# Residual stream turned to tokens on the partitions in a two-layer decoder trunk

## The chip, the core and the metric

The kernel runs on one NeuronCore of a Trainium2 chip. The core has engines that run side by side, each with a queue of its own: TensorE (PE in the profile; PEld is its loading of the stationary operand) multiplies matrices and writes to PSUM, VectorE (DVE) and ScalarE (ACT) do elementwise work, GpSimd (POOL) fills small tiles and can issue transfers, and SyncE (SP) issues transfers (DMA) between HBM and the on-chip memory SBUF. Engines wait for each other through semaphores. SBUF has 128 partitions; a tile is written here as partitions x elements. PSUM has eight banks of 512 fp32 numbers per partition, and here a bank holds one running sum.

A matrix product has a *stationary* operand of at most 128x128, which is loaded into the array, and a *moving* operand of up to 512 columns, which streams past it. The metric is device microseconds (us) of one execution; lower is better.

## The reference

A decoder trunk of two layers on 256 tokens of width 2048, all fp32. What matters here:

```
ALPHA = (2 * DEPTH) ** 0.25

def short_conv_mixer(x, w_in, conv_w, w_out):
    bcu = x @ w_in
    gate_b, gate_c, u = jnp.split(bcu, 3, axis=-1)
    v = gate_c * u
    y = lax.conv_general_dilated(...)
    return (gate_b * y) @ w_out

def sq_relu_mlp(x, w1, w2):
    return jnp.square(jax.nn.relu(x @ w1)) @ w2

for layer in range(DEPTH):
    if layer < N_A:
        mix = short_conv_mixer(h, ...)
    else:
        if layer == N_A:
            k_nope, k_pe, v = shared_latent_kv(h, ...)
        mix = mla_mixer(h, ..., k_nope, k_pe, v, cos, sin)
    h = layer_norm(ALPHA * h + mix, ln_g[layer, 0], ln_b[layer, 0])
    h = layer_norm(ALPHA * h + sq_relu_mlp(h, mlp_w1[layer], mlp_w2[layer]),
                   ln_g[layer, 1], ln_b[layer, 1])
return h
```

There is one layer of each kind, so there are four layer norms (0 to 3): after the convolution mixer, after the first MLP, after attention, after the second MLP. The MLP's hidden width is 8192. `w_out` (2048x2048), `w_o` (2048x2048) and the two `w2` (8192x2048) are called down projections here: their results are added to the residual stream.

## The kernel before

**Precision.** Every fp32 operand `a` of a large product is split into `hi`, a copy rounded to a faster format, and `lo = a - hi`; a product is the sum of hi·hi, hi·lo and lo·hi. ACT makes `hi` by a cast (L112 for weights, L198 for activations) and DVE makes `lo` by a subtraction (L113, L199). An activation tile has `hi` of 256 tokens in columns 0 to 255 and `lo` in columns 256 to 511.

**Layout.** Activations and the residual stream have features on the partitions and tokens in the columns: `xres` is 128 x 16 x 256. The stationary operand is a 128x128 weight block and the activations move. A *pair* (`mm_run`, L133 and L137) is one product of 512 columns (`hi` of the weight with both halves of the activation) and one of 256 (`lo` of the weight with `hi` of the activation); `mm` (L151 to L153) does the same in three products of 256 columns with one result of 256. Only the value projection of attention (L590 to L592) holds the activations (128 tokens) and moves 512 weight columns, three products for each block of inputs.

**Weights** come as one stream of 712 halves of 128x1024 (512 KB). `take` hands out the next halves and asks for splitting four halves ahead (`LOOK`). A half is loaded by SP into one of five `raw` buffers and split into one of eight `hi` and `lo` buffers (`whl`), which come free when the last product that reads them has ended.

**Order.** The program is written in one sequence; a scheduler of the framework orders the instructions of each engine, by the order of the text among those that are ready as it reckons, and places the semaphores. Each engine then runs its own list in that order and waits where an operand isn't ready. PSUM banks are taken from two pools of four, by turns: `Banks.next` counts the requests and takes the pool `pmm` where the count modulo 8 is under 4 and the second pool otherwise.

**Stages.** Convolution mixer (48 units of `w_in`); `w_out` with norm 0; the first MLP in eight eighths (`NQ`), each of 8 units of `w1` and then the down projection of these 1024 hidden features for all 2048 outputs; the key, value and query latents (9 units); attention in four groups of four heads, with the projections of the next group interleaved and the first units of `w_o` beside the last; the rest of `w_o` with norm 2; the second MLP; norm 3 and output.

**Layer norm before.** While outputs of a down projection are added to `xres` (`add`, L354, after `residual`), each 128-feature chunk is counted into running sums (`count`) and at once scaled by its gain and split into `xd` (`wide`, L286 and L287), not yet normalised. The next stage's first products, `mm_wide` (L164 to L166, 258 columns: 256 tokens and the gain and bias columns), start on `xd`. Mean and variance come from small products (`stats`, L296), and the normalisation is applied to the results of the products (`weighted`, L343 to L345), beside the normalising of `xres` itself (`normal`, L331 to L336). To keep numbers small a mean over the first chunk is subtracted beforehand (`prepare`, `mu0p`, L256). At the end (`to_out`) chunks are transposed on PE (L707) and normalised with a last product (L739).

## Time and profile before

| | us |
|---|---|
| median of 3 runs | 2080.92 (2079.13 to 2081.73) |
| the profiled execution | 2080.19 |
| its span, first to last instruction | 2078.4 |
| mean granted TensorE clock | 0.998 of full |

The profile is of one execution. Its page lists, for each engine, the time that it was busy and its share of the span; a chain of waits, which is followed back from the last instruction to what released each step; and groups of instructions, one line each: source line, engine, operation, output<-inputs, partitions x elements, how many, then busy time, mean ns of one, and idle time of the engine just before them with what ended it. A table of stretches gives, for each stretch `from:to` in us, its length and the busy time of each engine with the number of instructions, then the granted clock, the share of the DMA engines and GB/s. A timeline row is: start us, duration us, engine, line, operation, tiles, form, count. Products of PE are pipelined: one starts before the one ahead has left the array, so distances between starts are prices and durations are not.

### The profile page before, as it was taken

Reading aid. Unit: us, or ns where it says so; the run is one execution under the profiler, and the core shown is the slowest. Engines: PE = TensorE matmul, PEld = TensorE weight load, DVE = VectorE, ACT = ScalarE, POOL = GpSimd, SP = SyncE. Lnnn points to the kernel's source line nnn. Section 1 sums busy time; section 2 is a strip of 40 time slices with the busy share of each in tenths; the row PEclk is TensorE's granted clock in tenths of the full one; section 3 lists DMA queues with packets and bytes.
Section 4 is the critical chain, followed back from the end, with each engine's and each line's share of the span. In section 5 each row is a group of like instructions: output and inputs, shape, how many; then the busy total and the mean of one; then the engine's idle time right before and its main releaser. Section 6 shows DMA issues by size and latency. Waiting matters only on the chain.

```text
span 2078.4 us, 32534 instructions
## 1 busy us (share of the span) xinstructions
PE 2068.4 (100%) x12640; PEld 1841.6 (89%) x12640; DVE 1512.2 (73%) x2490; ACT 1010.8 (49%) x1473; POOL 2.2 (0%) x21
## 2 busy tenths in 40 slices
PE   9999999999999999999999999999999999999998
PEld 8888888988888888888899998898888888888898
DVE  7667677886676767667788878788667676676776
ACT  6444445654444443444456665565444444444354
POOL 0000000000000000000000000000000000000000
PEclk9999999999999999999999999999999999999999
DMA  8555555555555556565555444556555555555551
GB/s 312 196 186 189 190 185 188 176 193 187 191 191 193 188 179 202 190 189 190 192 183 173 133 142 143 188 167 202 190 188 190 193 190 187 192 192 190 188 183 62
DMA packets 107447, 383.42 MB, mean 184 GB/s; under 512 B 11927, under 2 KB 13335, under 8 KB 107287
## 3 DMA queue, kind: packets, MB, share of 16 engines
q1 hardware_dynamic: 107148, 381.09, 56.1%
q8 instruction: 99, 1.62, 0.3%
q14 instruction: 56, 0.45, 0.1%
q10 hardware_dynamic: 144, 0.26, 0.0%
HBM read 379.20 MB, written 2.10 MB: 183 GB/s over the span
## 4 chain that ended last, share of the span: by engine, by line
PE 98%; DVE 1%; DMA 0%; ACT 0%; issue 0%; DVEq 0%; ACTq 0%
PE ps_u L133 51%; PE ps_u L137 25%; PE ps_g L133 3%; PE ps_w L166 2%; PE ps_w L164 2%; PE ps_w L165 2%; PE ps_g L137 1%; PE ps_u L152 1%; PE ps_u L151 1%; PE ps_u L153 1%; PE S L612 0%; DMA xres<-in_xT_dram 0%; PE S L611 0%; PE ps_q L153 0%; PE ps_q L152 0%; PE ps_q L151 0%
## 5 line engine op out<-in xcount | busy, mean ns | idle before, releaser
L112 ACT CAST hi<-raw 128x1024 fp32r<-128x1024 f32 x712 | 747.7, 1053 | 909.1 <-PE ps_u L133 775.6
L113 DVE TENSOR_TENSOR lo<-raw,hi 128x1024 fp32r<-128x1024 f32 x712 | 870.4, 1224 | 366.6 <-ACT hi L112 344.0
L133 PE MATMUL ps_u<-xhl,hi 128*128 128x512 f32 x2512 | 874.8, 394 | 0.0
L137 PE MATMUL ps_u<-xhl,lo 128*128 128x256 f32 x2512 | 698.0, 278 | 0.0
L133 PEld LDWEIGHTS ps_u<-xhl,hi 128*128 128x128 f32 x2512 | 471.1, 188 | 110.1
L133 PE MATMUL ps_u<-h,hi 128*128 128x512 f32 x1568 | 544.2, 394 | 0.0
L137 PEld LDWEIGHTS ps_u<-xhl,lo 128*128 128x128 f32 x2512 | 472.2, 188 | 0.1
L137 PE MATMUL ps_u<-h,lo 128*128 128x256 f32 x1568 | 434.3, 277 | 0.0
L133 PEld LDWEIGHTS ps_u<-h,hi 128*128 128x128 f32 x1568 | 294.0, 188 | 68.3
L137 PEld LDWEIGHTS ps_u<-h,lo 128*128 128x128 f32 x1568 | 294.3, 188 | 0.0
L354 DVE TENSOR_TENSOR xres<-xres,ps_u 128x256 f32<-128x256 f32 x422 | 177.2, 420 | 116.2 <-PE ps_u L137 99.9
L166 PE MATMUL ps_w<-xd,hi 128*128 128x258 f32 x400 | 113.3, 284 | 0.0
L164 PE MATMUL ps_w<-xd,hi 128*128 128x258 f32 x400 | 113.2, 283 | 0.0
L165 PE MATMUL ps_w<-xd,lo 128*128 128x258 f32 x400 | 112.9, 282 | 0.0
L133 PE MATMUL ps_u<-z,hi 128*128 128x512 f32 x256 | 90.6, 399 | 0.0
L133 PE MATMUL ps_g<-h,hi 128*128 128x512 f32 x224 | 78.3, 394 | 0.0
L164 PEld LDWEIGHTS ps_w<-xd,hi 128*128 128x128 f32 x400 | 76.3, 191 | 0.1
L166 PEld LDWEIGHTS ps_w<-xd,hi 128*128 128x128 f32 x400 | 75.7, 190 | 0.0
L165 PEld LDWEIGHTS ps_w<-xd,lo 128*128 128x128 f32 x400 | 75.2, 188 | 0.0
L133 PE MATMUL ps_u<-oT,hi 128*128 128x512 f32 x208 | 73.5, 399 | 0.0
L137 PE MATMUL ps_u<-z,lo 128*128 128x256 f32 x256 | 71.7, 281 | 0.0
L198 ACT CAST h<-fh 128x256 fp32r<-128x256 f32 x128 | 51.5, 402 | 36.6 <-DVE fh L431 36.6
(211 smaller groups left out, 2091.2 us busy)
## 6 DMA issues: line engine op xcount, KB each, us to landing
raw<-in_w_dram SPq DMA_DIRECT2D x512, 512.0 KB, 4.1
raw<-in_w_in_dram SPq DMA_DIRECT2D x90, 512.0 KB, 3.4
raw<-in_w_out_dram SPq DMA_DIRECT2D x32, 512.0 KB, 3.3
raw<-in_w_o_dram SPq DMA_DIRECT2D x32, 512.0 KB, 3.4
raw<-in_w_kv_dram SPq DMA_DIRECT2D x10, 512.0 KB, 4.2
raw<-in_w_q_dram SPq DMA_DIRECT2D x8, 512.0 KB, 3.4
raw<-in_w_uk_dram SPq DMA_DIRECT2D x8, 512.0 KB, 3.3
raw<-in_w_qn_dram SPq DMA_DIRECT2D x8, 512.0 KB, 3.3
```

The lines of the kernel that those rows point to most:

```text
L112: nc.scalar.copy(hi[:, at, :], rv)
L113: nc.vector.tensor_tensor(lo[:, at, :], rv, hi[:, at, :].bitcast(F32), ALU.subtract)
L133: nc.tensor.matmul(ps, w[blk // 8][0][:, blk % 8, :], x, start=first, stop=False)
L137: nc.tensor.matmul(ps[:, :T], w[blk // 8][1][:, blk % 8, :], x[:, :T], start=False, stop=last)
L151: nc.tensor.matmul(ps[:, :T], lo, x[:, :T], start=first, stop=False)
L152: nc.tensor.matmul(ps[:, :T], hi, x[:, T:], start=False, stop=False)
L153: nc.tensor.matmul(ps[:, :T], hi, x[:, :T], start=False, stop=last)
L164: nc.tensor.matmul(ps[:, :W], hi, xd[:, k, :W], start=k == 0, stop=False)
L165: nc.tensor.matmul(ps[:, :W], lo, xd[:, k, :W], start=False, stop=False)
L166: nc.tensor.matmul(ps[:, :W], hi, xd[:, k, W:], start=False, stop=k == NC - 1)
L198: nc.scalar.copy(dst[:, :T], src)
L354: nc.vector.tensor_tensor(d, d, ps[:, :T], ALU.add)
```

## The change

- The residual stream is `res`, 128 tokens x 2 halves x 2048 features; it is loaded from a second copy of the input, by POOL, during the convolution.
- Down projections (`down`) hold the activations and move the weights: for each block of 512 output features (`NB` = 4) and each half of the tokens (`t`) one bank sums `dot`s of three products of 512 columns. Weights are laid out for it (`_rows`); the number of halves is the same. In the last block of the last down projection before a norm, the last four weight halves are held (`TAIL`), and token half 0 is summed before token half 1.
- `Norm.behind` adds a finished bank to `res` and takes statistics of the 512 columns with `bn_stats`; after the fourth block `finish` makes mean and reciprocal deviation per token. `normal` normalises 512 columns in place: one ACT operation and two on DVE with gain and bias, which POOL broadcasts to all partitions by DMA (`gb`).
- Before the next up projection, `turned` normalises, transposes on PE and splits each 128 x 512 block, and after both token halves of a block runs its 4 x 3 pairs for the first three weight units (`group_of(GROUP)`).
- `mm_wide`, `xd`, `weighted`, `prepare`, `count`, `stats`, `spread` of the norms and `to_out` are gone. The latents use ordinary pairs and `whole`.
- The last eighth's down projection no longer uses the three products of 256 columns, and `w_o`'s part beside attention is one block of 512 outputs in place of three units of 128.
- The first three weight units come in one transfer for each cut (`w_first`), `xT` chunks are split two at a time, and four constants are loaded by POOL.

```diff
+CUTS = (0, 2, 4, 8, 12, 16)
+TAIL = 4
+    def group_of(n, nk=NC):
+        return [(take(nk // 8), psum("ps_g")) for _ in range(n)]
+    def dot(ps, w, kk, x, k, t, nk):
+        hi, lo = (v[:, 4 * kk:4 * kk + 4, :].rearrange("p a c -> p (a c)") for v in w)
+        xh, xl = (x[:, k, o + t * P:o + (t + 1) * P] for o in (0, T))
+        nc.tensor.matmul(ps, xh, hi, start=k == 0, stop=False)
+        nc.tensor.matmul(ps, xh, lo, start=False, stop=False)
+        nc.tensor.matmul(ps, xl, hi, start=False, stop=k == nk - 1)
+
+    def down(x, nk, put, blocks=range(NB), last=False):
+        for n in blocks:
+            ps = [psum("ps_d") for _ in range(2)]
+            late = TAIL if last and n == NB - 1 else 0
+            for j in range(nk // 2 - late):
+                w, = take(1)
+                for kk in range(2):
+                    for t in range(2):
+                        dot(ps[t], w, kk, x, 2 * j + kk, t, nk)
+            ws = [take(1)[0] for _ in range(late)]
+            for t in range(2):
+                for i, w in enumerate(ws):
+                    for kk in range(2):
+                        dot(ps[t], w, kk, x, nk - 2 * late + 2 * i + kk, t, nk)
+                put(n, t, ps[t])
...
+    res = act.tile([P, 2, D], F32, tag="res", name="res")
+    def first_add(n, t, ps):
+        nc.vector.scalar_tensor_tensor(block(n, t), block(n, t), ALPHA, ps, ALU.mult, ALU.add)
+    def add(n, t, ps):
+        nc.vector.tensor_tensor(block(n, t), block(n, t), ps, ALU.add)
     class Norm:
-        def prepare(self, m):
-        def count(self, m):
-        def widen(self):
-        def wide(self, m):
-        def stats(self):
-        def weighted(self, ps, f):
...
+        def __init__(self, idx):
+            self.idx = idx
+            self.stats = small.tile([P, 2, NB, 6], F32, tag="stats", name=f"stats{idx}")
+            self.gb = act.tile([P, NB, 2 * BW], F32, tag="c", name=f"gb{idx}")
+            for n in range(NB):
+                nc.gpsimd.dma_start(self.gb[:, n, :], gb[idx, n].partition_broadcast(P))
+            self.rn = {}
+        def behind(self, put):
+            def go(n, t, ps):
+                put(n, t, ps)
+                nc.vector.bn_stats(out=self.stats[:, t, n, :], in_=block(n, t))
+                if n == NB - 1:
+                    self.finish(t)
+            return go
+        def finish(self, t):
+            mv = small.tile([P, 2], F32, tag="mv", name="mv")
+            nc.vector.bn_aggr(out=mv, in_=self.stats[:, t, :, :])
+            ve = small.tile([P, 1], F32, tag="ve1", name="ve1")
+            nc.vector.tensor_scalar(ve, mv[:, 1:2], LN_EPS, None, ALU.add)
+            rn = small.tile([P, 2], F32, tag="rn", name="rn")
+            rsqrt(rn[:, 0:1], ve)
+            nc.vector.scalar_tensor_tensor(rn[:, 1:2], mv[:, 0:1], -1.0, rn[:, 0:1], ALU.mult, ALU.mult)
+            self.rn[t] = rn
+        def normal(self, n, t):
+            r, g, b = block(n, t), self.gb[:, n, :BW], self.gb[:, n, BW:]
+            rn = self.rn[t]
+            u = tmp.tile([P, BW], F32, tag="u", name="u")
+            nc.scalar.activation(u, r, AF.Identity, bias=rn[:, 1:2], scale=rn[:, 0:1])
+            nc.vector.tensor_tensor(u, u, g, ALU.mult)
+            nc.vector.tensor_tensor(r, u, b, ALU.add)
+        def turned(self, dst, ws):
+            for n in range(NB):
+                for t in range(2):
+                    self.normal(n, t)
+                    ps = psum("turned")
+                    for j in range(4):
+                        nc.tensor.transpose(ps[:, j * P:(j + 1) * P], block(n, t)[:, j * P:(j + 1) * P], id_t)
+                    at = slice(4 * n, 4 * n + 4)
+                    hi, lo = (dst[:, at, o + t * P:o + (t + 1) * P] for o in (0, T))
+                    split(hi, lo, ps.rearrange("p (j c) -> p j c", c=P))
+                mm_run(ws, dst, 4 * n, 4 * n + 4, NC)
...
-    summed(ln, products(NC, z), residual, ln.wide)
+    ln = Norm(0)
+    down(z, NC, ln.behind(first_add), last=True)
+    def mlp(idx, ln):
         xhl = act.tile([P, NC, 2 * T], F32R, tag="b", name=f"xhl{idx}")
+        ws = group_of(GROUP)
+        ln.turned(xhl, ws)
         for q in range(NQ):
-            h = act.tile([P, QC, 2 * T], F32R, tag="c", name=f"h{idx}_{q}")
+            h = act.tile([P, QC, 2 * T], F32R, tag="a", name=f"h{idx}_{q}")
+            for m, ps in enumerate(products(QC, xhl, ws=() if q else ws)):
...
+            if q < NQ - 1:
+                down(h, QC, add if q else first_add)
             else:
+                ln = Norm(idx)
+                down(h, QC, ln.behind(add), last=True)
+        return ln
...
+    ln = Norm(2)
+    put = ln.behind(first_add)
+    for t in range(2):
+        put(0, t, first_o[t])
     banks = Banks.open("second")
+    down(oT, H, put, blocks=range(1, NB), last=True)
+    ln = mlp(3, ln)
+    for t in range(2):
+        for n in range(NB):
+            ln.normal(n, t)
+            nc.sync.dma_start(out[t * P:(t + 1) * P, n * BW:(n + 1) * BW], block(n, t))
```

467 lines of the change are left out of this document (110 added, 357 removed).

## The prediction

> **What bounds the kernel now.** I read the page's engine table and chain of waits first, then the groups of PE instructions, then the table of stretches, one stretch for each stage of the code.
>
> ```profile
> span 2078.4 us, 32534 instructions
> PE 2068.4 (100%) x12640; PEld 1841.6 (89%) x12640; DVE 1512.2 (73%) x2490; ACT 1010.8 (49%) x1473; POOL 2.2 (0%) x21
> PE 98%; DVE 1%; DMA 0%; ACT 0%; issue 0%; DVEq 0%; ACTq 0%
> L133 PE MATMUL ps_u<-h,hi 128*128 128x512 f32 x1568 | 544.2, 394 | 0.0
> ```
>
> TensorE (PE) is never idle and is 98% of the chain, so a change is worth what it does to PE's sequence: how long each product takes, and whether PE must ever stand still. The 394 ns of a product is its passage through a pipeline, not its price; prices have to come from starts and from stretches.
>
> ```profile
> core 0: us, PE busy (x) PEld busy (x) DVE busy (x) ACT busy (x) POOL busy (x), PEclk, DMA share, GB/s
> 277.10:367.70 90.60, 90.60 (x515) 78.36 (x514) 68.70 (x111) 46.60 (x65) 0.00 (x0) 1.00 0.56 186
> 367.70:415.20 47.50, 47.50 (x399) 47.50 (x398) 39.31 (x75) 31.61 (x55) 0.00 (x0) 1.00 0.54 173
> 503.90:548.30 44.40, 44.40 (x259) 38.83 (x258) 32.82 (x49) 17.45 (x18) 0.00 (x0) 1.00 0.61 190
> 1036.80:1082.90 46.10, 46.10 (x387) 46.10 (x386) 41.43 (x78) 28.27 (x48) 0.00 (x0) 1.00 0.56 183
> 1082.90:1136.80 53.90, 53.90 (x453) 53.90 (x452) 45.75 (x89) 34.96 (x63) 0.00 (x0) 1.00 0.55 177
> 1346.50:1393.90 47.40, 47.40 (x399) 47.40 (x398) 39.61 (x75) 31.76 (x55) 0.00 (x0) 1.00 0.55 178
> 2015.60:2063.50 47.90, 47.90 (x402) 47.75 (x402) 33.81 (x59) 23.44 (x42) 0.00 (x0) 1.00 0.17 57
> ```
>
> In order: the `w_out` product; the first "wide" group (norm 0, with the statistics inside it); one ordinary down projection of an MLP eighth (128 pairs of one 512-column and one 256-column product); the last eighth's down projection in three 256-column products; the nine wide latent units; the wide group of norm 2; the last down projection of all. PE is full in each: **the norms cost the old kernel no standstill**, because the products start on un-normalised columns.
>
> **Part one, down projections.** Per four 128x128 weight blocks the old form has eight products and 3072 moving columns, the new one six of 512 columns, the same 3072. The new form is in the trace already, in the value projection (L590 to L592); two starts of its second column block:
>
> ```profile
> 1149.18 0.39 PE L592 MATMUL ps_v<-hi,lat 128*128 128x512 f32 x1
> 1153.95 0.39 PE L592 MATMUL ps_v<-hi,lat 128*128 128x512 f32 x1
> ```
>
> They lie 21 products apart: 4.77/21 = 0.2271 us each. So an eighth costs 192 x 0.2271 = 43.6 against 44.4 (saves 0.8, 14 times: 11.2); the two last eighths 43.6 against 46.1 and 47.9 (2.5 + 4.3); `w_out` 384 x 0.2271 = 87.2 against 90.6 (3.4), `w_o` taken like it (3.4). **Saved: 24.8.** The other bound is the neighbouring form's rate, 44.4/192 = 0.2313: then only the last eighths and the two long products gain, 24.8 - 3840 x 0.0042 = 8.7.
>
> **Part two, wide products.** They become ordinary pairs, 128 for 44.4 us, 144 for 49.9: saves 47.5 - 44.4, 47.4 - 44.4 and 53.9 - 49.9 = **10.1**. The centring products on the ones matrix go too:
>
> ```profile
> L256 PE MATMUL mu0p<-xres,ones 128*128 128x256 f32 x8 | 2.5, 391 | 0.0
> ```
>
> Between 0 and 2.5, taken 1.3, since the durations of neighbours overlap.
>
> **Part three, three norms in the open.** In the new `mlp` and before the latents, PE has nothing to do between the last product of a down projection and the first transposed block: `turned` needs the finished statistics. The rows nearest to its steps (512 columns, of which some are known at 256 or 1024):
>
> ```profile
> L112 ACT CAST hi<-raw 128x1024 fp32r<-128x1024 f32 x712 | 747.7, 1053 | 909.1 <-PE ps_u L133 775.6 <-issue 65.2 <-PE ps_g L133 19.8
> L113 DVE TENSOR_TENSOR lo<-raw,hi 128x1024 fp32r<-128x1024 f32 x712 | 870.4, 1224 | 366.6 <-ACT hi L112 344.0
> L113 DVE TENSOR_TENSOR lo<-first,hi 128x512 fp32r<-128x512 f32 x9 | 5.7, 688 | 0.0
> L112 ACT CAST hi<-first 128x512 fp32r<-128x512 f32 x9 | 5.0, 618 | 0.0
> L333 ACT ACTIVATE xres<-nu,vec 128x256 f32<-128x256 f32 x48 | 28.6, 600 | 8.6 <-DVE nu L332 8.5
> L618 DVE TENSOR_REDUCE mx<-kqv 128x1 f32<-128x256 f32 x16 | 6.5, 409 | 0.0
> L618 DVE TENSOR_REDUCE mx<-kqv 128x1 f32<-128x128 f32 x16 | 4.5, 279 | 0.1
> 1090.04 0.16 DVE L304 SCALAR_TENSOR_TENSOR ve<-stat,ve 128x2 f32<-128x2 f32 x1
> 1090.23 0.17 DVE L227 RECIPROCAL iv<-ve 128x2 f32<-128x2 f32 x1
> 1090.31 1.23 DVE L113 TENSOR_TENSOR lo<-raw,hi 128x1024 fp32r<-128x1024 f32 x1
> 1091.45 0.15 DVE L229 TENSOR_TENSOR rt<-sq,iv 128x2 f32<-128x2 f32 x1
> 1092.04 0.16 DVE L312 TENSOR_TENSOR nr<-nm,rr 128x2 f32<-128x2 f32 x1
> 2063.62 0.74 PE L707 MATMUL turned<-id_t,fin 128*128 128x128 f32 x5
> ```
>
> VectorE's (DVE's) 512-column operation is 0.69; the statistics instruction appears nowhere, and a reduction grows by 0.13 for 128 columns, so 0.67 (bounds 0.4 and 1.2: faster reading, or two passes). ScalarE (ACT) with scale and bias: 0.60 + 256 x 0.84 ns = 0.82. The chain after the square root is taken over as it stands here, 1090.04 to 1092.20 = 2.2, with a weight split slipped into its gap. A transpose is about 0.11.
>
> Until the first product after a norm: end of the last product 0.2, a split already on DVE 0.5 (half of one), sum 0.69, statistics 0.67, aggregation 0.2, chain 2.2, ACT 0.82 plus half a split in the way 0.5, two DVE operations 1.3, four transposes and their way to PSUM 0.7, cast 0.6, subtraction 0.7, and DVE's work for the other token half in between 1.5: **10.6**. The four splits fall there because `whl` has eight buffers: the four tail halves free theirs only while token half 1 is summed, and `group_of(3)` asks for ten halves. The five-microsecond tail covers token half 0's statistics, not half 1's.
>
> After that, PE does four runs of 12 pairs (16.6, part of the 44.4 already counted) and 24 more transposes, 2.6. DVE needs 6 x 0.61 = 3.7 per run and splits besides, PE 4.2 + 0.9, so PE is nearly the longer one; but transposes queue behind the run before them, and what follows them is then uncovered, 0.7 + 0.6 + 0.7 = 2.0: once in each norm. In norms 0 and 1 the bank counter puts the three open sums and transposed tiles five to eight in the same pool of four banks: those tiles share **one** bank, each waiting for the subtraction before it. That adds up to three such waits; I take two. In norm 2 the counter stands at 6 and banks are free.
>
> Then the clock:
>
> ```profile
> 2066.50:2068.50 2.00, 0.15 (x2) 0.16 (x3) 1.43 (x11) 0.51 (x3) 0.00 (x0) 1.00 0.00 0
> 2068.50:2070.50 2.00, 1.99 (x10) 1.23 (x8) 0.52 (x1) 1.14 (x3) 0.00 (x0) 0.81 0.00 0
> 2070.50:2072.50 2.00, 2.00 (x7) 1.34 (x7) 0.98 (x2) 0.60 (x1) 0.00 (x0) 0.50 0.63 235
> 1.05 3.77 PE L212 MATMUL warm<-ones 128*128 128x128 f32 x16 [1.05 <-DVE col L214]
> ```
>
> Some 2 us of near idleness at the end of the old kernel brought the granted clock to 0.81 and 0.50, while the sixteen warm-up products ran at 0.24 each, twice a transpose's price, for 3.8 us. A norm's 8 us without products should do the same. Half of 3.8 is 1.9 lost; the queueing waits hide part: I take 1.0 in norms 0 and 1, 1.5 in norm 2.
> The Trainium skill ("TensorE: Matmul & The Clock Gate", Part 1) states that an idle window of about 3.4 us halves the clock and a busy one restores it, which speaks against this change three times over; by it a restart would lose, as an estimate, 1.7 to 3.4, so 5 to 10 in all against my 3.5.
>
> Norms 0 and 1: 10.6 + 2.6 + 2.0 + 4.0 + 1.0 = 20.2 each; norm 2: 10.6 + 2.6 + 2.0 + 1.5 = 16.7; together 57. Floor: without the two half splits, the one in the chain (0.9) and a third of half 0's work (0.5) it is 8.2 + 2.6 = 10.8 each, 32 in all. Ceiling: two more splits in the way and all three bank waits everywhere, 10.6 + 2.4 + 2.6 + 2.0 + 6.0 = 23.6 each, 71. The steps were added as if none lay beside another and the middle of the bounds is 52: I take **53**.
>
> **Part four, the ends and the queues.** Now 14.9 us pass from the last down product (2063.5) to the span's end.
>
> ```profile
> 2073.03 1.61 DVE L743 TENSOR_SCALAR fin<-turned,rr 128x512 f32<-128x512 f32 x2 [1.44 <-PE turned L739]
> out_dram<-fin SPq DMA_DIRECT2D x8, 256.0 KB, 2.4
> 5.00:24.00 19.00, 17.31 (x93) 14.34 (x94) 14.28 (x33) 13.09 (x33) 0.00 (x0) 1.00 1.01 375
> ```
>
> New: DVE has the sum, statistics and chain of half 1 (2.6 without splits) and, of eight normalised blocks at 1.22, six or seven still to do: 0.2 + 2.6 + 7.9 = 10.7, then from DVE's last end (2074.6) to the span's end as now, 3.8: 14.5, **saved 0.4**. The start is bound by transfers (share 1.01 at 375 GB/s) and moves the same bytes with fewer issues: 0, between -1 and +1. Gains and biases come as four broadcast transfers of 512 KB for each norm, 8.4 MB, and the token-major input another 2.1, all issued by POOL, behind whose queue only the 2-column memsets wait; each has 40 us or more before its use; the four constants move to it from SP's queue, where they stood among the weight loads; and the weights take 190 of the 375 GB/s. So nothing; without cover 2.1/0.375 = 6 us for a norm. Sums into the residual take 8 DVE operations of 0.69 instead of 32 of 0.42 for an eighth, off the path.
>
> Sum: -24.8 - 10.1 - 1.3 - 0.4 + 53 = **+16.4**. Against the profiled execution's 2080.19 (span 2078.4 and 1.8 around it) that is 2096.6; the median, 2080.92, stands 0.7 higher: **2097**.
>
> **Rivals.**
> *Norms at their floor.* If token half 0 is normalised in the tail and no split stands before half 1's chain, the three norms cost 32 against 36.6 saved: 2076, and with the centring and start terms at their better ends 2074. For it: DVE is 73% busy, with slack before the tail. Against: the row at 1090.31, where a split entered the chain the moment DVE was free. It decides if the first pair after a norm starts within 8 us of the last down product; from 12.2 us per norm down the kernel is not slower.
> *Moving the weights gains nothing per column.* That the change doesn't do what it says: 0.2313 instead of 0.2271 for 3840 products adds 16, 2113. For it: `w_out`'s pairs need 90.6/256 = 0.354 where others need 0.347, so a slower rhythm exists. Against: 21 products in a row at 0.2271.
> *Norms at their ceiling*, DVE the bound through the whole of `turned`: 71, 2115; DVE is already at 83% (39.31 of 47.5) in the stretch this replaces, and ACT's casts wait in order on PE for buffers (775.6 us of idle time in its row).
>
> **Chances.** Forecast (2086 to 2106) 0.50; floor 0.25; slow products 0.12; ceiling 0.13. What a measurement of this kernel can tell from no change is about 0.2%, 4 us. Of the floor's share 0.18 is faster than that and 0.07 within it; of the forecast's tails 0.02 each: faster 0.20, same 0.09, slower 0.71. The range for eight in ten is 2073 to 2114; the likeliest case alone 2086 to 2106.
>
> **What would show it.** Products of `ps_d` 0.227 apart; `turned` lines with PE idle for 8 to 11 us three times, released by DVE; a granted clock below 1 just after; DVE nearly full there; 14 to 15 us from the last product to the end. I am wrong in sign if PE's idle time in the three norms is under 30 us in sum, and in size if an eighth's down projection isn't 43.6.

## The result, and the profile after

| | before | after |
|---|---|---|
| median, us | 2080.99 (4 runs, 2079.13 to 2081.73) | 2114.51 (4 runs, 2111.84 to 2118.53) |
| ratio after/before | | 1.0164, 95% interval 1.0143 to 1.0185 |
| span of the profiled execution, us | 2078.4 | 2115.1 |
| mean granted clock | 0.998 | 0.987 |

The kernel became slower by 33.5 us in the medians and by 36.7 between the two profiled executions. The direction was the forecast's (2097 us), the size about twice its +16.4, and the median lies half a microsecond over its range of 2073 to 2114.

The page of the kernel after: the span, the busy time of the engines, and the chain of waits.

```profile
span 2115.1 us, 27698 instructions
PE 2065.5 (98%) x10698; PEld 1760.6 (83%) x10698; DVE 1313.0 (62%) x1820; ACT 940.2 (44%) x1271; POOL 14.0 (1%) x43
PE 96%; DVE 2%; DMA 1%; issue 1%; ACT 0%; SPq 0%; DVEq 0%
```

PE issues 1942 products fewer, yet its busy time falls by 3 us only, and DVE, at 62% instead of 73%, was relieved without effect. The totals hide where the time went; the table of stretches shows it, cut at the same seams in both kernels. First the stretches of the kernel before that the prediction didn't show: the first group, the convolution units, an up projection, the MLP stages with all their eighths, attention.

```profile
core 0: us, PE busy (x) PEld busy (x) DVE busy (x) ACT busy (x) POOL busy (x), PEclk, DMA share, GB/s
5.30:24.50 19.20, 17.77 (x96) 14.71 (x97) 14.48 (x33) 13.29 (x32) 0.00 (x0) 1.00 0.99 368
24.50:277.10 252.60, 252.60 (x1444) 219.93 (x1443) 173.23 (x255) 116.62 (x157) 1.41 (x14) 1.00 0.61 202
459.50:503.90 44.40, 44.40 (x258) 38.84 (x257) 28.11 (x39) 20.86 (x30) 0.00 (x0) 1.00 0.59 190
415.20:1082.90 667.70, 667.70 (x3972) 589.98 (x3972) 481.42 (x743) 306.83 (x407) 0.00 (x0) 1.00 0.59 190
1136.80:1346.50 209.70, 209.42 (x1336) 189.04 (x1336) 169.88 (x370) 120.33 (x226) 0.00 (x0) 1.00 0.46 151
1393.90:2063.50 669.60, 669.60 (x3989) 591.50 (x3988) 473.65 (x723) 301.76 (x400) 0.00 (x0) 1.00 0.55 180
```

And the kernel after, in order of time: first group, convolution units, `w_out`, norm 0 with the first up projection, a down and an up projection, the whole first MLP from there, norm 1 with the latents, attention with `w_o`, norm 2, the second MLP, the end (columns as above).

```profile
7.00:31.80 24.80, 20.63 (x97) 17.25 (x98) 14.87 (x26) 13.26 (x25) 0.14 (x2) 0.93 0.95 379
31.80:286.20 254.40, 254.40 (x1443) 220.55 (x1442) 167.09 (x235) 115.12 (x155) 1.41 (x14) 1.00 0.64 197
286.20:373.20 87.00, 87.00 (x386) 71.88 (x384) 47.34 (x54) 34.95 (x36) 2.11 (x4) 1.00 0.67 207
373.20:434.90 61.70, 52.81 (x290) 44.99 (x290) 45.35 (x74) 31.32 (x48) 2.09 (x4) 0.89 0.53 183
434.90:478.40 43.50, 43.50 (x194) 36.02 (x193) 24.47 (x26) 17.44 (x18) 0.00 (x0) 1.00 0.66 197
478.40:523.60 45.20, 45.20 (x257) 39.16 (x256) 28.28 (x39) 20.81 (x30) 0.00 (x0) 1.00 0.64 188
434.90:1099.90 665.00, 665.00 (x3330) 562.57 (x3328) 397.86 (x486) 285.31 (x355) 0.00 (x0) 1.00 0.62 189
1099.90:1167.80 67.90, 59.59 (x328) 50.89 (x327) 50.24 (x86) 36.27 (x60) 0.00 (x0) 0.90 0.45 147
1167.80:1373.70 205.90, 205.73 (x1206) 181.88 (x1204) 140.34 (x283) 105.21 (x187) 2.09 (x4) 1.00 0.54 161
1373.70:1434.70 61.00, 51.33 (x289) 44.41 (x289) 45.46 (x72) 31.43 (x48) 2.09 (x4) 0.89 0.59 188
1434.70:2099.60 664.90, 664.90 (x3330) 562.64 (x3328) 392.39 (x483) 279.59 (x350) 0.00 (x0) 1.00 0.60 181
2099.60:2115.10 15.50, 0.37 (x2) 0.00 (x0) 11.05 (x24) 4.98 (x7) 0.00 (x0) 0.61 0.36 135
```

Set side by side (the three norms against the wide groups shown ahead of the prediction):

| stage | before | after | change | forecast |
|---|---|---|---|---|
| until the first group has ended | 24.5 | 31.8 | +7.3 | 0 |
| convolution units | 252.6 | 254.4 | +1.8 | -1.3 |
| `w_out` | 90.6 | 87.0 | -3.6 | -3.4 |
| norms 0, 1, 2 with their up projections | 47.5, 53.9, 47.4 | 61.7, 67.9, 61.0 | +41.8 | 53 - 10.1 = +42.9 |
| rest of the two MLPs | 667.7, 669.6 | 665.0, 664.9 | -7.4 | -18.0 |
| attention and `w_o` | 209.7 | 205.9 | -3.8 | -3.4 |
| end | 14.9 | 15.5 | +0.6 | -0.4 |
| sum | | | +36.7 | +16.4 |

The norms, the one large and uncertain term, came out as forecast in sum. The miss of 20 us is elsewhere: 7.3 at the start, some 11 in the MLPs, 3 in the convolution units, all costed at nothing or at the old price.

**The MLPs.** The down projections do as forecast, 43.5 instead of 44.4. The up projections, which the diff doesn't touch, take 45.2 instead of 44.4 in all fourteen places. PE's timeline of the kernel after, a little after the down projection's last product at 478.20 (start, duration, instruction):

```profile
479.11 0.40 PE L133 MATMUL ps_u<-xhl,hi 128*128 128x512 f32 x1
479.35 0.28 PE L134 MATMUL ps_u<-xhl,lo 128*128 128x256 f32 x1
...
480.88 0.40 PE L133 MATMUL ps_u<-xhl,hi 128*128 128x512 f32 x1
```

and of the kernel before, at the start of the same up projection:

```profile
459.53 0.39 PE L133 MATMUL ps_u<-xhl,hi 128*128 128x512 f32 x1
...
461.26 0.40 PE L133 MATMUL ps_u<-xhl,hi 128*128 128x512 f32 x1
```

Five pairs lie between the first and the last row in both: 1.77/5 = 0.354 us each after, 1.73/5 = 0.346 before. PE isn't idle, no wait is shown, and the clock is 1.00: the same pair simply has two rhythms. Times 128 the difference is 0.9 for an up projection, the 0.8 of the table, and some 12 us for fourteen. The convolution units run at the slow rhythm from end to end.

**The start.** The timeline of POOL's queue, and two groups of transfers (KB each, us to landing):

```profile
1.25 1.19 POOL L335 DMA_DIRECT2D res<-in_xt_dram  x2 [0.80 <-POOLq L624]
...
4.02 0.54 POOL L337 DMA_DIRECT2D mask_t<-in_mask_dram  x1
first<-in_w_first_dram SPq DMA_DIRECT2D x3, 768.0 KB, 16.1
xraw<-in_xT_dram SPq DMA_DIRECT2D x3, 512.0 KB, 14.7
```

In the text of the kernel the input copy is loaded in the convolution loop and the four constants after it. Nothing in the data holds them there, and the scheduler put all six at the head of POOL's list. Their 2.6 MB share 379 GB/s with the weights on which the first group waits: 2.6/0.379 = 6.9 us of the 7.3.

**A norm.** Three stretches of norm 0: from the last `w_out` product to the first transposes, on to the first pair, and the first twelve pairs.

```profile
373.20:379.30 6.10, 0.27 (x2) 0.05 (x1) 6.03 (x12) 2.40 (x4) 0.00 (x0) 0.71 0.71 234
379.30:385.70 6.40, 3.34 (x13) 2.14 (x13) 5.28 (x13) 4.39 (x8) 0.00 (x0) 0.50 0.30 90
385.70:391.60 5.90, 5.90 (x24) 5.08 (x25) 5.56 (x9) 2.83 (x4) 0.00 (x0) 0.69 0.00 0
```

12.5 us without a pair, and the granted clock falls to 0.50, so that the next twelve pairs take 5.9 instead of 4.2. DVE is full (6.03 of 6.10). Six rows of its timeline there, with others between them left out:

```profile
374.24 0.16 DVE L265 SCALAR_TENSOR_TENSOR rn<-mv,rn 128x1 f32<-128x1 f32 x1
374.32 1.23 DVE L106 TENSOR_TENSOR lo<-raw,hi 128x1024 fp32r<-128x1024 f32 x1
375.47 0.68 DVE L233 SCALAR_TENSOR_TENSOR res<-res,ps_d 128x512 f32<-128x512 f32 x1
376.67 0.69 DVE L253 BATCH_NORM_STATS2 stats<-res 128x6 f32<-128x512 f32 x1
377.27 1.21 DVE L106 TENSOR_TENSOR lo<-raw,hi 128x1024 fp32r<-128x1024 f32 x1
380.14 0.16 DVE L265 SCALAR_TENSOR_TENSOR rn<-mv,rn 128x1 f32<-128x1 f32 x1
```

The two rows of L265 are the results of token halves 0 and 1. Half 1's sum (L233) waits behind a weight split for a product that ended at 373.3, and another split stands between its statistics and its result at 380.3, 7.0 us after the last product. From the first pair on PE stands still no more; 43 products of the later units stand between the runs of the turned blocks, where the scheduler put them. Twelve of the 32 transposes lie ahead of the first pair. So 12.5, the other 20 transposes (1.9), 1.7 lost to the clock and 1.2 more, mostly in the pairs of the later units, make the 17.3 by which 61.7 exceeds 44.4.

### The profile page after: what moved, and what is told of

Its sections match the earlier page's. It is cut to its first block, busy times and chain, and to the rows that moved or that the text cites. A ratio compares the mean times of both kernels' runs of the same rounds, so it can differ in the third digit from the quotient of the medians.

```text
span 2115.1 us, 27698 instructions
## 1 busy us (share of the span) xinstructions
PE 2065.5 (98%) x10698; PEld 1760.6 (83%) x10698; DVE 1313.0 (62%) x1820; ACT 940.2 (44%) x1271; POOL 14.0 (1%) x43
## 4 chain that ended last, share of the span: by engine, by line
PE 96%; DVE 2%; DMA 1%; issue 1%; ACT 0%; SPq 0%; DVEq 0%
PE ps_u L133 31%; PE ps_u L134 15%; PE ps_d L162 13%; PE ps_d L163 13%; PE ps_d L164 13%; PE ps_g L133 2%; PE ps_g L134 1%; DMA first<-in_w_first_dram 1%; PE S L487 1%; DVE u L274 1%; PE S L486 0%; DVE res L275 0%; PE ps_q L142 0%; PE ps_q L141 0%; PE ps_q L140 0%
## 5 line engine op out<-in xcount | busy, mean ns | idle before, releaser
L133 PE MATMUL ps_u<-xhl,hi 128*128 128x512 f32 x2768 | 979.0, 399 | 0.0
L134 PE MATMUL ps_u<-xhl,lo 128*128 128x256 f32 x2768 | 776.3, 281 | 0.0
L162 PE MATMUL ps_d<-hi,h 128*128 128x512 f32 x1024 | 398.8, 389 | 0.0
L164 PE MATMUL ps_d<-hi,h 128*128 128x512 f32 x1024 | 398.6, 389 | 0.0
L163 PE MATMUL ps_d<-lo,h 128*128 128x512 f32 x1024 | 398.4, 389 | 0.0
L164 PEld LDWEIGHTS ps_d<-hi,h 128*128 128x128 f32 x1024 | 192.2, 188 | 40.6
L162 PEld LDWEIGHTS ps_d<-hi,h 128*128 128x128 f32 x1024 | 192.2, 188 | 40.1
L163 PEld LDWEIGHTS ps_d<-lo,h 128*128 128x128 f32 x1024 | 192.2, 188 | 39.5
L133 PE MATMUL ps_g<-xhl,hi 128*128 128x512 f32 x192 | 76.8, 438 | 7.9 <-ACT hi L105 4.2
L236 DVE TENSOR_TENSOR res<-res,ps_d 128x512 f32<-128x512 f32 x112 | 71.9, 681 | 12.9 <-PE ps_d L164 12.9
L187 ACT COPY t<-ps_u 128x256 f32<-128x256 f32 x173 | 63.4, 366 | 4.1 <-PE ps_u L134 4.1
L134 PE MATMUL ps_g<-xhl,lo 128*128 128x256 f32 x192 | 56.9, 298 | 0.0
```

Source lines behind the costliest of these rows:

```text
L133: nc.tensor.matmul(ps, hi, x[:, k, :], start=k == 0, stop=False)
L134: nc.tensor.matmul(ps[:, :T], lo, x[:, k, :T], start=False, stop=k == nk - 1)
L162: nc.tensor.matmul(ps, xh, hi, start=k == 0, stop=False)
L163: nc.tensor.matmul(ps, xh, lo, start=False, stop=False)
L164: nc.tensor.matmul(ps, xl, hi, start=False, stop=k == nk - 1)
L187: nc.scalar.copy(t, ps[:, T:])
```

## The experiments

Times are of one run each where nothing else is said, beside runs of the kernel before on the same chip, which lay between 2076.3 and 2081.7 throughout. Spans compare with 2115.1 after and 2078.4 before. A single total can shift by the 4.8 us of the convolution's rhythm (shown below), so the readings rest on stretches.

### The start

`e1_late` ties the six transfers to the convolution's output by a one-column copy into their targets.

```diff
+            nc.vector.tensor_copy(res[:, m - 2, 0:1], y[:, 0:1])
             nc.gpsimd.dma_start(res[:, m - 2, :], xt[(m - 2) * P:(m - 1) * P, :])
...
+        nc.vector.tensor_copy(dst[:, 0:1], y[:, 0:1])
         nc.gpsimd.dma_start(dst, src)
```

> The token-major input and four constants are issued by POOL only once the convolution has produced chunks 2, 3 and 15 (a one-column copy in front of each transfer ties them to that). Theory A: the 2.5 MB were issued at 1.25 us of the changed kernel and shared the DMA engines with the first weights, which is why its first group of products ended at 31.8 us instead of 24.5; then the group ends at 24 to 25 and the whole gains 6.5 to 7.5 us. Theory B: the first weights come late because they are now few, larger transfers (one of 384 KB for three of 128 KB); then the group still ends at 30 or later and the gain is under 2 us.

2110.37 us, span 2108.6. The stretch of the first group, and the same weight transfer as above, in this run:

```profile
7.00:25.40 18.40, 18.35 (x97) 15.96 (x98) 14.78 (x26) 13.23 (x25) 0.14 (x2) 1.00 0.93 368
first<-in_w_first_dram SPq DMA_DIRECT2D x3, 768.0 KB, 9.7
```

The group ends at 25.4 instead of 31.8, the landing takes 9.7 instead of 16.1 us, and the clock stays at 1.00 (0.93 in the kernel after). The span falls by 6.5, and 6.4 of it are here. The start's loss is the moved transfers, less the 0.9 that separates 25.4 from the old kernel's 24.5, whose cause no run isolates.

### The rhythm of the pairs

`e2_entry` puts throwaway products ahead of the up projections of single eighths. Their results are overwritten.

```diff
             ps = psum("ps_u")
+            if i == 0:
+                kick(ps, w, x, extra)
             mm_run([(w, ps)], x, 0, nk, nk)
```

> Between a down projection and the next up projection stand throwaway products into the bank that the first real product then clears: in the first MLP none, one of 256 columns, two of 256, one of 128, one fp32 product of 128, one fp32 of 256, one of 512 for eighths 1 to 7; in the second two fp32 of 128, three of 256, one of 64, two of 128, one of 384, four fp32 of 128, none. Theory A: the pairs of an up projection run at 0.353 or at 0.347 us by the place in a short cycle at which they are entered, and the new down projections always enter at the slow place; then some of the fourteen take 44.4 us and a few tenths, those with none 45.2, and which ones depends on the columns put in. Theory B: the rhythm comes from where operands lie in memory or from what else runs beside; then all fourteen keep 45.2 plus their throwaway products.

2109.67 us. From one down projection to the next, throwaway products included (the kernel after has 88.8 everywhere):

| throwaway products | us | | throwaway products | us |
|---|---|---|---|---|
| none | 88.8 | | one fp32, 256 columns | **88.4** |
| one fp32r, 64 columns | 88.9 | | one fp32, 128 | 89.0 |
| one, 128 | 88.9 | | two fp32, 128 | **88.4** |
| one, 256 | 88.9 | | four fp32, 128 | 88.8 |
| one, 384 | 89.0 | | two, 256 | 89.0 |
| one, 512 | 89.0 | | three, 256 | 89.1 |
| two, 128 | **88.1** | | | |

(fp32r is the format of `hi` and `lo`.) Two fp32r products of 128 columns turn the up projection fast, one of 256 with as many columns doesn't, so what decides is not the columns; this run doesn't say what it is. Four fp32 products were also followed by fast pairs, but cost 0.8 themselves.

`e5_kick` has two products of 128 columns ahead of all fourteen, and ahead of the convolution units, with the late transfers.

> Late transfers as in the run before, and two throwaway products of 128 columns ahead of the first conv unit after the group and ahead of the up projections of eighths 1 to 7 in both MLPs. Theory A (the price of a pair, 0.3534 or 0.3465 us, is a rhythm that is set where a run of pairs is entered, and depends on nothing else): conv units 249.6 instead of 254.4, each of the fourteen up projections 44.6 with its throwaway products instead of 45.2, so some 13 us less than the run with late transfers alone, 2097. Rival B (pairs after 512-column weight-moving products stay slow, and the two fast ones seen were accidents of one place): fewer than seven of the fourteen are fast, and the throwaway products cost 14 x 0.25 = 3.5: 2110 or more.

2101.36 us, span 2099.6, so 9.0 less than `e1_late`. One up projection with its throwaway products:

```profile
472.40:517.00 44.60, 44.60 (x260) 39.04 (x259) 28.26 (x39) 20.83 (x30) 0.00 (x0) 1.00 0.64 189
```

All fourteen take 44.6 instead of 45.2, and the two MLPs are 9.3 us shorter in sum. The convolution units stayed slow (254.6), so theory A is right that the entry sets the rhythm, and wrong that this one key fits every entry: behind other pairs it did nothing.

The convolution's rhythm varies by itself. Over nine runs of kernels whose instructions are the same up to the first norm, the units took 249.6 us five times (`e2_entry`, `e4_nostat`, `e7_warm2`, `e9_hold`, `e14_pool`) and 254.4 four times (`e3_warm`, `e6_look`, `e13_nogain` and the kernel after). The four times of the kernel after, 2111.84 and 2112.19 against 2116.82 and 2118.53, lie as far apart; that this is why wasn't shown.

`e8_beforekick` and `e10_beforekick2` do the like to the kernel before, in convolution, `w_out` and `w_o`; the edit of the second:

```diff
+            if i == group + 1 and n > QC and group != 2:
+                nc.tensor.matmul(ps[:, :T], ones, xres[:, 0, :], start=True, stop=True)
             if halves:
                 mm_run([(w, ps)], x, 0, nk, nk)
```

> The kernel before, with two throwaway products ahead of the first conv unit after the group (fp32), ahead of w_out and ahead of w_o (fp32r, 128 columns). Theory A (one rhythm for both kernels, set at the entry): the slow stretches of the kernel before turn fast: conv to the centring product 133.1 instead of 135.7, w_out 88.8 instead of 90.6, w_o 72.2 instead of 73.5, in sum 5.7 less, 2075. Rival B (the slow stretches of the kernel before have their own cause, such as their transfers): no change, 2081.

> The kernel before, with one throwaway fp32 product of 256 columns (like the centring product after which its conv stage turned fast) ahead of the second free unit of conv, of w_out and of w_o. Two fp32r products of 128 columns did not turn the pairs of w_out and w_o (90.7 and 73.7, slow), though the same turned all fourteen up projections of the kernel after. Theory A (out of a slow run of pairs the fp32 product leads to the fast rhythm): w_out some 89.0 and w_o 72.4 with the throwaway product, 3 us less than the same kernel without. Rival B (these stretches have a slow rhythm of their own): 90.9 and 73.8, nothing gained, 0.4 lost.

2077.85 and 2076.76 us. `w_out` took 90.7 with the first, as slow as ever, and in the second run:

```profile
275.00:364.40 89.40, 89.40 (x516) 78.53 (x515) 68.42 (x111) 46.57 (x65) 0.00 (x0) 1.00 0.59 188
```

89.4 with the throwaway product inside, and `w_o`'s pairs 72.6 instead of 73.5. So the slow stretches of the old kernel are the same rhythm. In the convolution both runs were fast up to the centring product (133.1 behind two fp32 products of 128 columns, 133.9 behind one of 256, instead of 135.7). Out of a slow run of pairs one fp32 product of 256 columns led to the fast one, here in `w_out` and `w_o`, and in the old kernel at its centring product, behind which the pairs turn from 0.353 to 0.346. The convolutions of these two runs and of `e12_best` count for less, since that stage changes its rhythm by itself.

`e15_beforekick2` is that kernel timed.

> The kernel before with one fp32 throwaway product in conv, w_out and w_o, again, timed. In one look w_out took 89.4 instead of 90.5 and w_o 72.5 instead of 73.4 with the throwaway products inside. Theory A (the rhythm is worth 2.0 there, and up to 2.3 in conv when conv would run slow): 2 to 4 us under the kernel before, ratio 0.998 to 0.999. Rival B (conv's rhythm varies from run to run in both, and hides it): ratio 1.000.

2077.49 us (11 runs, 2076.63 to 2079.14) against 2078.79 (15 runs, 2076.32 to 2081.50): ratio 0.9995, interval 0.9986 to 1.0004. The 2 us in the stages are too little to be told from no change.

### What a norm's 17 us are

`e4_nostat` leaves out the norms' statistics and scales by a constant 0.7.

```diff
-                nc.vector.bn_stats(out=self.stats[:, t, n, :], in_=block(n, t))
-                if n == NB - 1:
-                    self.finish(t)
...
-            nc.scalar.activation(u, r, AF.Identity, bias=rn[:, 1:2], scale=rn[:, 0:1])
+            nc.scalar.activation(u, r, AF.Identity, bias=0.0, scale=0.7)
```

> Leaves out the statistics of all four norms: each block is scaled by 0.7 in place of its token's reciprocal deviation and mean, then gain and bias as before; transposes, splits and the order of blocks stay. Theory A: the norms' time is mostly the chain from the last sum to the normalised block, in which weight splits stand; without it the stretch from the last down product to the next down projection shrinks from 61 to 62 us to 50 to 55, and the end from 15.5 to about 11. Theory B: DVE's sum of work in the stretch sets it; then it shrinks by no more than the 3 us of statistics work.

2077.68 us, span 2075.5. Norm 0 to its first pair, and to the next down projection:

```profile
368.10:372.20 4.10, 1.87 (x17) 1.63 (x15) 4.10 (x6) 3.52 (x6) 0.00 (x0) 0.98 0.90 342
368.10:420.40 52.30, 50.03 (x290) 43.71 (x289) 33.48 (x49) 24.96 (x39) 2.09 (x4) 0.97 0.63 208
```

The first pair comes after 4.1 us instead of 12.5, and the norms take 52.3, 59.1 and 53.5 instead of 61.7, 67.9 and 61.0: 25.7 less, of which 23.3 are the earlier first pairs. Theory A held. The mean clock of norm 0 is 0.97 instead of 0.89, but it still falls to 0.72 for the first pairs: in norms 0 and 2 twelve of them take 5.8 and 5.9, in norm 1 4.3. The rest of the 39.6 is the end (6.8 instead of 15.5), the convolution, fast in this run (4.8), and 0.4 at the start. So the wait for the statistics is half of what the norms cost over ordinary up projections (51.9 in sum). It is more than the statistics' own operations: without them the earlier blocks are normalised while the last one is still being summed.

`e13_nogain` keeps the statistics and leaves out gains and biases, two of three elementwise steps of each block.

```diff
-            nc.scalar.activation(u, r, AF.Identity, bias=rn[:, 1:2], scale=rn[:, 0:1])
-            nc.vector.tensor_tensor(u, u, g, ALU.mult)
-            nc.vector.tensor_tensor(r, u, b, ALU.add)
+            nc.scalar.activation(r, r, AF.Identity, bias=rn[:, 1:2], scale=rn[:, 0:1])
```

> The kernel after without the gains and biases of the norms: ScalarE's scale and bias by token write the residual directly, VectorE's two operations of 0.69 us for each block are left out (16 of them in a norm, 11 us of VectorE). Theory A (what stays of a norm without its statistics, some 9 of 17 us, is VectorE working block by block): each norm 4 to 9 us cheaper, the first product after a norm 9.5 to 11 us from the last dot, the end 5 us shorter; total 2088 to 2101 against 2112 to 2117. Rival B (it is PE's own order: transposes, pairs and banks): 1 to 2 us per norm, 2107 or more.

2104.43 us, span 2102.7; the norms 58.9, 65.6 and 59.7, the end 9.7.

```profile
373.40:384.00 10.60, 3.73 (x18) 2.67 (x17) 7.37 (x16) 8.91 (x14) 0.00 (x0) 0.64 0.65 197
```

Counted from the end of the last product in both runs, the first pairs come 2.1, 2.1 and 2.4 us sooner, and 3.0, 2.5 and 1.5 us are gained in the norms. The first pairs (9.2 to 10.3 us) and the end are theory A's; the gain of a norm lies between the theories, nearer to rival B. DVE's 11 us of gain and bias count only where they stand ahead of the first pair. Later blocks are hidden by pairs.

`e14_pool` gives the bias to GpSimd.

```diff
-            nc.vector.tensor_tensor(r, u, b, ALU.add)
+            nc.gpsimd.tensor_tensor(r, u, b, ALU.add)
```

> The kernel after with the bias of the norms added by GpSimd instead of VectorE, 8 operations of 512 columns in each norm. Theory A (VectorE bounds the blocks, and GpSimd has nothing else to do there): 2 to 5 us less per norm if GpSimd's operation takes under 1 us; total 2100 to 2110. Rival B (GpSimd's operation is longer than VectorE's 0.69 and stands in each block's chain): the norms get longer, 2116 or more.

2126.87 us, rival B.

```profile
L275 POOL TENSOR_TENSOR res<-u,gb 128x512 f32<-128x512 f32 x32 | 42.7, 1340 | 1623.0 <-DVE u L274 1521.7 <-DVE ve L262 99.3 <-issue 2.0
```

GpSimd takes 1.34 us where DVE takes 0.69. The first pair of norm 0 comes 16.2 us after the last product, and the norms take 65.4, 71.3 and 65.2.

**The clock.** `e3_warm` and `e7_warm2` fill the standstill with throwaway fp32 products of 256 columns that read the just added block: 26 and 12, then 14 and 5.

```diff
+            keep(block(NB - 1, 0), 14)
...
+                    if n == 0 and t == 0:
+                        keep(block(0, 0), 5)
```

> In each of the three norms 26 throwaway fp32 products of 256 columns follow the last down product and 12 more the first transposes, so that PE isn't idle while it waits. Theory A: the halved clock after a norm's wait (transposes at 0.24, the first six pairs at 0.64 us) comes from PE's idleness; then the granted clock stays at 1.00, the first twelve pairs take 4.2 instead of 6.0 us, and each norm gains 1.8 to 3 us, 5 to 9 in all. Theory B: the clock falls whatever the throwaway products do, or they only delay the transposes; then no norm gains more than 0.5 us.

> Fewer throwaway products than in the run that kept the clock by 26 and 12: 14 fp32 ones of 256 columns (6.0 us at full clock) after the last dot, 5 (2.2 us) after the first turned block. Theory A (the lowered clock is worth 2 to 3 us at each norm, and the throwaway products of the first attempt cost more because they stood ahead of the transposes): first product of the turned group no later than 12.5 us from the last dot, its 12 pairs in 4.2 instead of 6.0: 2 to 3 us less at each norm, total 2106 to 2110. Rival B (DVE's chain, not the clock, sets the times of the stage, and the pairs then wait for the next turned block): less than 1 us at each norm, 2112 to 2117.

The first took 2134.25 us: its products run 0.43 us each, 11.2 and 5.2 in all, and held the transposes back, so that the first pair came 18.9 us after the last product. The second took 2107.93, of which the convolution's fast rhythm gives 4.8 against the profiled kernel after:

```profile
368.40:380.80 12.40, 10.07 (x51) 8.19 (x49) 11.21 (x24) 6.44 (x10) 0.00 (x0) 1.00 0.52 160
380.80:385.20 4.40, 4.40 (x26) 3.82 (x26) 4.33 (x8) 2.91 (x5) 0.00 (x0) 1.00 0.02 4
```

The first pair stands where it stood (12.4), so the chain of DVE and ACT sets it; the clock is 1.00 throughout, and the first twelve pairs take 4.4 instead of 5.9. Norms 0 and 1 took 59.5 and 65.5, 2.2 and 2.4 less. Part of that may be chance: in the kernel after, `e1_late`, `e2_entry` and `e5_kick`, which leave the norms alone, they took 60.5 to 61.6 and 67.3 to 67.9, so the gain is 1.0 to 2.2 and 1.8 to 2.4. `e12_best` repeats it (59.4 and 65.4). Norm 2 took 61.4, nothing less: there PE stood idle for 0.7 and 1.9 us between the throwaway products and the first pair, and the first twelve pairs took 5.7 at a clock of 0.72. In norm 0 idle stretches of 0.6 and 1.8 us left the clock at 1.00; why the two differ isn't shown.

**The splits in the chain.** `e6_look` asks for the lookahead of the turned group's weights later; `e9_hold` ties their transfers to token half 1's result.

```diff
+            if i in state.get("hold", ()):
+                nc.vector.tensor_copy(raw[:, 0:1], state["rn"][:, 0:1])
             nc.sync.dma_start(raw, stream[i])
```

> The group that opens each normed product asks for its own six weight halves only; the four halves of lookahead are asked for one by one between the runs of the turned blocks. Theory A (VectorE's splits of weight halves, 1.23 us each, stand in the chain of statistics: four lie between the first and the last token half's chain): the first product after each norm comes 2.5 to 5 us sooner (after norm 0 at 8 to 10 us from the last dot instead of 12.5), the clock drops for less time, the three norms cost 40 to 46 instead of 52; total 2102 to 2109 against 2115. Rival B (the splits only fill gaps that the chain leaves; what counts is the chain itself): within 1 us per norm, 2113 to 2118, or slower where a half then comes late.

> The deferred lookahead moved only one of the four weight splits that stand in VectorE's chain of statistics, since nothing held their transfers. Here the transfers of weight halves six to ten of each normed group are tied to the second token half's result (a one-column copy into their buffers), so that one split of 1.23 us is left in the chain. Theory A (three splits in the way make the chain longer): the first product of the turned group 7.5 to 9.5 us from the last dot instead of 12.5, each norm 2 to 5 us cheaper, total 2100 to 2109 against 2115. Rival B (work that only moves: the same splits, and loads that start late, are then missing among the turned blocks): the first product comes sooner, but the stage ends within 1 us of where it did: 2112 to 2117.

The first took 2118.55 us, with the first pair 0.6 later in norms 0 and 1: three of the splits stayed in the chain and the fourth moved behind one step of it, since the scheduler, held by no dependence, pulled them up again. In the second (2112.78 us, with the convolution in its fast rhythm) they were gone, and half 1's result came 5.0 instead of 7.0 us after the last product. Yet the first pair came at 11.8, 11.4 and 11.9 instead of 12.4, 11.4 and 12.1, and the norms took 60.7, 69.2 and 61.2, nothing less in sum. Four rows of DVE's timeline in that run, from the result to the first pair at 381.0, with others between them left out:

```profile
374.03 0.16 DVE L267 SCALAR_TENSOR_TENSOR rn<-mv,rn 128x1 f32<-128x1 f32 x1
377.73 0.68 DVE L276 TENSOR_TENSOR u<-u,gb 128x512 f32<-128x512 f32 x1
379.15 1.23 DVE L106 TENSOR_TENSOR lo<-raw,hi 128x1024 fp32r<-128x1024 f32 x1
380.29 0.68 DVE L106 TENSOR_TENSOR xhl<-turned,xhl 128x512 fp32r<-128x512 f32 x1
```

The subtraction that releases the first pair (380.29) now stands in DVE's list behind the normalising of two later blocks and a split. Rival B held: the work moved, and the order filled the room. An order in which the first block goes through to its pairs before the next is normalised wasn't tried.

### Do the pieces add up?

`e11_all` joins late transfers, throwaway products at the up projections and in the convolution (one fp32), tied weight transfers, and 2 and 8 products in the norms; `e12_best` leaves the tied transfers out and takes 14 and 5.

> All in one, on the kernel after: late transfers, throwaway products ahead of the fourteen up projections, an fp32 one ahead of the second free conv unit, tied transfers of halves six to ten, and 2 and 8 throwaway fp32 products in each norm. Theory A (separate causes that add up): -6.5 (start) - 9.0 (up projections) - 4.5 (conv, if its rhythm was slow) - 2 each for the clock and 2 to 5 each for the splits in three norms, so 2080 to 2090. Rival B (the norm stage is bound by its own chain of turned blocks, whatever stands ahead of it): start and rhythm alone, 2095 to 2100.

> The kernel after with late transfers, throwaway products ahead of the up projections and in conv, and 14 and 5 throwaway fp32 products in the norms, without the tied weight transfers, which lengthened the norms of the run with all (58.0, 69.5 and 64.1 against 59.5, 65.5 and 61.4 us with the 14 and 5 alone). Theory A (the pieces add up): 2097.2 - 5.2 = 2092, a ratio of 1.005 to the kernel before. Rival B (the norms in that run were slow for another reason): 2096 or more.

`e11_all` took 2097.23 us, in rival B's range: its norms were 58.0, 69.5 and 64.1. The first pairs came 1.9 to 2.6 us sooner, and the late weights cost more afterwards (PE waited 2.9 us for DVE in norm 1). `e12_best` took **2093.70 us** (4 runs, 2093.50 to 2095.09), ratio 1.0074 to the kernel before, interval 1.0060 to 1.0088, nearer to theory A. Its norms:

```profile
364.00:423.40 59.40, 57.07 (x327) 49.56 (x326) 45.14 (x74) 31.23 (x48) 2.08 (x4) 1.00 0.55 187
1083.80:1149.20 65.40, 63.54 (x366) 55.28 (x365) 50.00 (x86) 36.18 (x60) 0.00 (x0) 1.00 0.47 155
1355.10:1415.90 60.80, 58.20 (x327) 50.60 (x326) 45.40 (x72) 31.37 (x48) 2.08 (x4) 0.97 0.58 189
```

Its span is 2091.7, 23.4 under the kernel after: 9.3 until `w_out` (start and convolution), 4.6 and 4.7 in the MLPs, 5.0 in the norms, within 0.2. What stays, 13.3 us over the old kernel's span, is in the main what the norms cost over the old wide groups (36.8) less what the MLPs, `w_out` and attention save (some 24). No version of the new kernel with complete norms beat the old one.

## Why the prediction was half right

- **Down projections, 0.2271 us a product: right.** 43.5 for an eighth, 87.0 for `w_out`; attention with `w_o` saved 3.8 for 3.4. The rival that moving the weights would gain nothing (0.2313) is out, though its 2113 lay next to the result. The rival with the norms at their ceiling came nearer still, at 2115, and is out too: they cost 51.9, not 71.
- **Norms, 53 us: right in sum (51.9), with errors that cancelled.** To the first pair 10.6 was forecast and 12.4, 11.4 and 12.1, counted from the end of the last product, were measured. The steps were sized well (512-column statistics 0.69 for 0.67, ACT 0.81 for 0.82). Splits stood in the chain as forecast. The 2.0 of uncovered transposes and the 4.0 of bank waits did not happen: through the turned blocks PE ran without a stop, in norms 0 and 1 with pairs of the later units between the turned blocks. The sign set for being wrong in direction, PE idle for under 30 us in the three norms, misled: the table's rows leave 26.9 idle, and the kernel was slower all the same, since transposes and pairs at a lowered clock count as busy.
- **The clock, 1.0 to 1.5 a norm: on the low side** in norms 0 and 1, where keeping it was worth 1.0 to 2.2 and 1.8 to 2.4. The estimate of 1.7 to 3.4 that the prediction worked out from the Trainium skill ("TensorE: Matmul & The Clock Gate", Part 1) overlaps these. In norm 2 nothing was gained by the products that kept it in the other two.
- **"0, between -1 and +1" for the start: wrong, +7.3.** The failed step is "So nothing" for the extra transfers. It asked when their data are used (40 us or more ahead) and not when they are issued: the input copy and the constants went out at the start, where the transfer engines were already full. The price that the prediction set beside it for a norm's gains, "without cover 2.1/0.375 = 6 us", is of the size of what the start lost to them (6.4).
- **"They become ordinary pairs, 128 for 44.4 us, 144 for 49.9": wrong as a fixed price.** The fourteen up projections that the change leaves alone were carried over at it, at no cost, and took 0.8 more each, some 12 us. The prediction had seen a slow rhythm in `w_out` (0.354) and laid it on the products that the change adds. It struck those that it leaves alone, since what runs ahead of them changed.
- **The end:** 14.5 forecast, 15.5 measured. `e4_nostat` puts the wait for the statistics at 8.7 of it.

With the start and the up projections (7.3 + 10.6 against the forecast), the convolution's rhythm (3.1) and the end (1.0), less 1.7 in the other terms, the miss of 20.3 us between the profiled executions is accounted for.

## What to carry to other kernels

A transfer without a dependence has no place in time: ask what holds it, and price it at the moment when the transfer engines are fullest. The price of an unchanged instruction sequence holds only behind the same neighbours; where a stage alternates two forms of product, look for both rhythms in the trace before one is multiplied by thousands. When a reduction over all outputs must end before the next stage can start, the chain behind the last output is the cost, and thinning it helps only if the engine's list doesn't put later blocks into the room.

## What was not expected of the hardware

- One pair of products (512 and 256 columns, each with its own weight load) has two rhythms, 0.3465 and 0.3534 us, at full clock and without waits. A run keeps the one that it enters with for as long as 250 us, the same instructions enter now with one and now with the other, and two products of 128 columns or one fp32 product of 256 can turn it. Why, stays open.
- Keeping PE busy with throwaway products cost nothing as long as they ended before the awaited operand came; 38 in place of 19 delayed the first pair by 6.4 to 7.5 us.
- GpSimd's addition of 512 columns takes 1.34 us against DVE's 0.69.
